# Two attention mixers of a two-layer encoder: logits, transposes and PV as separate steps, normalisation on ScalarE, alternating dilated slot pairs

## The chip, the core and the metric

The kernel runs on one core of a Trainium2 chip. The metric is the device time of one execution in microseconds. The kernel before takes 2126.91 us, the median of 3 runs (2126.51 to 2127.47).

The engines are named as in the profile: PE is TensorE (PEld its weight loads), DVE is VectorE, ACT is ScalarE, POOL is GpSimd, and SP is SyncE, whose queue issues nearly all DMAs.

## The reference

512 tokens of width 1024 go through two layers, everything in float32:

```python
for i in range(DEPTH):                                    # DEPTH = 2
    h = h + 0.5 * swiglu(rmsnorm(h, norm_ffn1[i]), ...)    # width 2816
    hn = rmsnorm(h, norm_mix[i])
    if i % 2 == 0: h = h + ab_mixer(hn, ...)               # layer 0
    else:          h = h + c_mixer(hn, ...)                # layer 1
    h = h + 0.5 * swiglu(rmsnorm(h, norm_ffn2[i]), ...)
    gate = sigmoid(rmsnorm(h, norm_ple[i]) @ w_ple_gate[i])
    h = h + gate * (p[i] @ w_ple_proj[i])
return rmsnorm(h, norm_final)
```

The mixer of layer 0 has two parts. Part A has 12 query heads on 4 key heads (64 wide), with rotary positions; a query sees the keys at a distance of at most 128, and each head has one further logit (a sink) in its softmax denominator. Part B has 4 slots, and each slot has three groups of dilated attention: distance up to 64 at stride 1, up to 256 at stride 4, and up to 1024 at stride 16. The outputs of the three groups of a slot are merged by their softmax denominators. The mixer of layer 1 is a neighbourhood attention with 16 heads: the tokens form a grid of 8 rows and 64 columns, and a query sees 8 x 16 grid cells, with a learned bias for each offset.

## The kernel before

**Layout and precision.** Activations lie with the features on the 128 partitions and the 512 tokens along the free dimension. Every float32 product of a weight matrix is made of three matmuls: operands are split into a high and a low part (`split`, lines 120 to 122: ScalarE copies the high part, VectorE or GpSimd subtracts it to get the low part), and `mm3` (lines 142 to 144) or lines 322 to 324 multiply high by high, high by low and low by high. A weight unit of 128 x 1024 is loaded on SyncE's queue and split in the same way (`unit`, lines 129 to 137).

**Buffers.** Long-lived tiles of 128 x 512 float32 come from the pool `act` with 59 buffers, short-lived ones from `tmp` with 8. PSUM has 3 banks `mm` for projections, 2 banks `sc` for scores, 2 banks `tr` for transposes and 1 bank `ob` for the PV output of a head. A tile is given out when a buffer of its pool is free, and it is free when its last reader is done.

**A head of the banded kind** (part A, and the stride-1 group of part B). The four query blocks of 128 tokens are b = 0 to 3. Block b sees the key blocks of `window(b)`, so blocks 0 and 3 have 256 keys and blocks 1 and 2 have 384. `scores` (lines 418 to 431) makes two matmuls a block and one VectorE instruction that scales, adds the mask and takes the row maximum. `a_soft` (559 to 573) then has ScalarE take the exponentials with their sums (line 568), VectorE add the sink and take the reciprocal (569, 570), and VectorE multiply every block by it (572). `windows_pv` (362 to 371) goes through the four key blocks x: it transposes the two or three logit blocks that see x (line 349, into one `tr` bank), splits the result (lines 121 and 122, ScalarE and VectorE), and makes the two PV matmuls of x (359 and 360). `half_sum` (677 to 683) adds the two halves of the output.

**The dilated part** goes by two pairs of slots. `b_steps` (575 to 675) has for a pair: `soft(0)` and `soft(1)` for its two slots (the stride-1 group as above, and the groups of stride 4 and 16 by residues, matmuls of line 598, exponentials of line 608); `merge`, which gathers the maxima and sums of both slots with 32 small copies (617 and 634), works out the merge weights and multiplies all 16 logit blocks of the pair by them on VectorE (line 638); `pv_r`, the transposes and PV of the residue groups (647 and 653); and `pv_n(0)`, `pv_n(1)`, the stride-1 group's transposes and PV.

**The neighbourhood mixer** goes by 8 head pairs: `c_soft` (785 to 812) makes scores, bias, exponentials and normalisation (VectorE, line 811); `c_pv` (814 to 836) twice transposes four blocks into one bank, splits them and makes their PV matmuls.

**The order of the work.** Each mixer writes two lists. `steps` holds the attention in order. `fill` holds the projections of queries, keys and values (and two opened parts of the output projection), which are dense TensorE work. Every entry has a weight. `weave` (lines 502 to 525) goes through the steps and puts fill entries between them: an entry comes when a step at most `lead` places further on needs it, or else when the weight of the fill done so far has fallen behind that of the steps done. The result is the program order, and program order is priority: a planner at build time goes by its own costs of the instructions, gives out buffers and lets a later instruction go ahead where an earlier one is not ready; each engine then runs its queue in the fixed order that comes out. `high_priority()` moves the instructions in it ahead. In the neighbourhood mixer `lead` is 2, in the first mixer 1. A step of a head's PV follows the logits of the next head, so that the program order is logits 0, logits 1, PV 0, logits 2, PV 1, and so on. In the first mixer the two slot pairs follow one after the other, and the last projections of the second pair stand among the PV steps of the first.

Of the kernel before, what the change touches and what calls it, by code (L numbers as in the profile page):

```python
# [15 lines left out]
P = 128  # L16
T = 512
# [19 lines left out]
class Trunk:  # L37
# [3 lines left out]
    def __init__(self, ctx, tc, io):  # L41
# [6 lines left out]
        self.ap_ = pool("act", 59)  # L48
        self.tp = pool("tmp", 8)
# [40 lines left out]
    def setup(self):  # L90
# [5 lines left out]
        self.identb = self.cp.tile([P, P], BF16, name="identb")  # L96
        nc.vector.tensor_copy(self.identb, self.ident)
# [7 lines left out]
        idle = self.cp.tile([P, T], BF16, name="idle")  # L105
# [237 lines left out]
    def transposed(self, blocks):  # L343
# [6 lines left out]
        hi, lo = self.tmp(F32R), self.tmp(F32R)  # L350
# [67 lines left out]
    def scores(self, q, k, hf, b, m):  # L418
# [6 lines left out]
        e = self.act()[:, :n]  # L425
# [5 lines left out]
        return e  # L431
# [5 lines left out]
    def ab(self, k_next):  # L437
# [94 lines left out]
    def a_steps(self, gp, t, v, m_a, sink, mix):  # L532

        heads = [(hf, j) for j in range(3) for hf in range(2)]
        es, raw = {}, {}

        def soft(hf, j):
            h = 6 * gp + 3 * hf + j
            es[hf, j] = self.a_soft(t["aq", gp, j], t["ak", gp], hf, sink[:, h:h + 1], m_a)

        def pv(hf, j):
            if hf == 0:
                raw[j] = self.act()
            g = 2 * gp + hf
            o = self.obank()
            self.windows_pv(o, es[hf, j], lambda x: v["va"][x][:, g * P:(g + 1) * P])
            self.half_sum(o, slice(hf * HD, (hf + 1) * HD), raw[j])
            if hf:
                mix[3 * gp + j] = self.split_chunk(raw[j])

        steps = []
        for i in range(len(heads) + 1):
# [509 lines left out]
```

## Time and profile before

| What | Value |
|---|---|
| Median of 3 runs | 2126.91 us |
| Profiled execution, its own time | 2126.64 us |
| Span of its instructions | 2124.8 us |
| Mean granted TensorE clock | 0.995 of full |
| First mixer, about | 380 to 660 us |
| Neighbourhood mixer, about | 1470 to 1670 us |
| DMA | 202 MB, 95 GB/s in the mean |

The profile is of one execution. A row of a group of instructions reads: line of the program, engine, operation, tiles written and read, shape, count; then busy time in us and the mean of one in ns; then the engine's idle time just before them, with what ended it. Consecutive matmuls overlap in the trace, so a mean of one matmul is longer than the distance from one to the next.

### The profile page before, as it was taken

How to read it: one execution, taken by the hardware profiler on the slowest of the kernel's cores; microseconds unless marked ns; L12 is line 12 of the kernel's file. 1: busy time of each engine (PE TensorE's matmuls, PEld its weight loads, DVE VectorE, ACT ScalarE, POOL GpSimd, SP SyncE). 2: the span in 40 equal slices, each digit the busy share in tenths (PEclk: the TensorE clock that was granted, in tenths of full speed). 3: DMA queues.
4: the chain of work that ended last, by engine and by line, in shares of the span. 5: the costliest groups of instructions: out<-in, count | busy, mean ns of one | idle time of the engine just before them, and what ended most of it. 6: DMA issues, size and time to landing. Idle time of an engine off the chain costs nothing.

```text
span 2124.8 us, 25520 instructions
## 1 busy us (share of the span) xinstructions
PE 2085.4 (98%) x9950; PEld 1734.6 (82%) x9950; DVE 1132.3 (53%) x1793; ACT 783.8 (37%) x1255; POOL 352.3 (17%) x248
## 2 busy tenths in 40 slices
PE   8999999999999999999999999999999999999998
PEld 6888888777787888888888888888888888888886
DVE  6554432699786444543354555333778744553334
ACT  4332222465544333222343233223656533232232
POOL 3111101233211111101111111013222210110111
PEclk9999999999999999999999999999999999999999
DMA  5333333221223233333333322334333223323331
GB/s 171 98 99 99 95 96 98 85 75 56 65 68 92 90 99 99 99 90 96 105 97 99 99 93 93 95 97 124 105 105 102 82 90 99 99 91 96 94 107 60
DMA packets 75385, 202.02 MB, mean 95 GB/s; under 512 B 16896, under 2 KB 24576, under 8 KB 75264
## 3 DMA queue, kind: packets, MB, share of 16 engines
q1 hardware_dynamic: 74976, 200.29, 30.8%
q8 instruction: 78, 1.28, 0.3%
q14 instruction: 43, 0.35, 0.1%
q10 hardware_dynamic: 288, 0.10, 0.0%
HBM read 191.97 MB, written 2.59 MB: 92 GB/s over the span
## 4 chain that ended last, share of the span: by engine, by line
PE 89%; DVE 5%; ACT 2%; issue 1%; POOL 1%; DMA 0%; SPq 0%; DVEq 0%; POOLq 0%; ACTq 0%
PE mm L143 15%; PE mm L144 15%; PE mm L142 15%; PE sc L142 12%; PE sc L143 12%; PE sc L144 12%; PE mm L322 1%; PE mm L323 1%; PE mm L324 1%; PE tr L349 1%; PE ob L359 1%; PE ob L360 1%; PE sc L428 1%; ACT wh L121 1%; DVE act L572 1%
## 5 line engine op out<-in xcount | busy, mean ns | idle before, releaser
L121 ACT ACTIVATE wh<-wr 128x1024 fp32r<-128x1024 f32 (+1 forms) x360 | 374.6, 1042 | 995.0 <-issue 431.1
L122 DVE TENSOR_TENSOR wl<-wr,wh 128x1024 fp32r<-128x1024 f32 (+1 forms) x343 | 510.2, 1488 | 314.1 <-ACT wh L121 313.1
L143 PE MATMUL mm<-act,wh 128*128 128x512 f32 (+1 forms) x1560 | 609.7, 391 | 3.0 <-DVE act L169 2.1
L142 PE MATMUL mm<-act,wh 128*128 128x512 f32 (+1 forms) x1560 | 609.1, 391 | 1.0 <-ACT wh L121 0.6
L144 PE MATMUL mm<-act,wl 128*128 128x512 f32 (+1 forms) x1560 | 608.3, 390 | 0.5 <-DVE wl L122 0.5
L144 PE MATMUL sc<-act,wl 128*128 128x512 f32 (+1 forms) x1138 | 442.5, 389 | 0.8 <-DVE wl L122 0.8
L142 PE MATMUL sc<-act,wh 128*128 128x512 f32 (+1 forms) x1138 | 442.9, 389 | 0.0
L143 PE MATMUL sc<-act,wh 128*128 128x512 f32 (+1 forms) x1138 | 442.5, 389 | 0.0
L143 PEld LDWEIGHTS mm<-act,wh 128*128 128x128 f32 x1560 | 293.4, 188 | 64.4 <-DVE act L169 5.3
L142 PEld LDWEIGHTS mm<-act,wh 128*128 128x128 f32 x1560 | 293.3, 188 | 60.0 <-ACT act L121 1.5
L144 PEld LDWEIGHTS mm<-act,wl 128*128 128x128 f32 x1560 | 293.2, 188 | 58.4 <-DVE wl L122 1.0
L239 POOL TENSOR_TENSOR tmp<-tmp,tmp 128x512 f32<-128x512 f32 x88 | 115.2, 1309 | 818.5 <-DVE tmp L238 783.7
L144 PEld LDWEIGHTS sc<-act,wl 128*128 128x128 f32 x1138 | 213.7, 188 | 45.1 <-DVE wl L122 1.2
L143 PEld LDWEIGHTS sc<-act,wh 128*128 128x128 f32 x1138 | 213.7, 188 | 44.1
L142 PEld LDWEIGHTS sc<-act,wh 128*128 128x128 f32 x1138 | 213.6, 188 | 43.8
L238 DVE TENSOR_TENSOR tmp<-sc,R 128x512 f32<-128x512 f32 x88 | 60.8, 691 | 276.8 <-PE sc L144 276.8
L180 POOL TENSOR_TENSOR ssq<-ssq,tmp 128x512 f32<-128x512 f32 x55 | 90.2, 1639 | 552.6 <-ACT tmp L175 525.7
L236 DVE TENSOR_TENSOR tmp<-mm,R 128x512 f32<-128x512 f32 x88 | 60.8, 691 | 130.4 <-PE mm L144 127.9
L121 ACT ACTIVATE act<-tmp 128x512 fp32r<-128x512 f32 x92 | 58.3, 634 | 117.3 <-POOL tmp L239 116.2
L322 PE MATMUL mm<-wh,act 128*128 128x256 f32 x256 | 74.4, 291 | 0.3 <-DVE act L337 0.3
L323 PE MATMUL mm<-wl,act 128*128 128x256 f32 x256 | 73.9, 289 | 0.0
L324 PE MATMUL mm<-wh,act 128*128 128x256 f32 x256 | 73.8, 288 | 0.0
(142 smaller groups left out, 1621.8 us busy)
## 6 DMA issues: line engine op xcount, KB each, us to landing
wr<-in_gu_dram SPq DMA_DIRECT2D x176, 512.0 KB, 3.5
wr<-in_dn_dram SPq DMA_DIRECT2D x64, 512.0 KB, 3.5
wr<-in_dn_dram SPq DMA_DIRECT2D x32, 384.0 KB, 3.1
wr<-in_qk_ab_dram SPq DMA_DIRECT2D x20, 512.0 KB, 3.5
wr<-in_plg_dram SPq DMA_DIRECT2D x16, 512.0 KB, 3.5
wr<-in_qk_c_dram SPq DMA_DIRECT2D x16, 512.0 KB, 3.7
act<-act SPq DMA_DIRECT2D x40, 128.0 KB, 2.2
wr<-in_v_ab_dram SPq DMA_DIRECT2D x8, 512.0 KB, 3.8
```

Source lines behind the costliest of these rows:

```text
L121: self.nc.scalar.activation(hi, src, AF.Copy)
L122: (lo_eng or self.nc.vector).tensor_tensor(lo, src, hi.bitcast(F32), op=ALU.subtract)
L142: mm(out, stat[0], mov[0], start=start, stop=False)
L143: mm(out, stat[0], mov[1], start=False, stop=False)
L144: mm(out, stat[1], mov[0], start=False, stop=stop)
L180: eng.tensor_tensor(self.acc, self.acc, sq, op=ALU.add)
L236: nc.vector.tensor_tensor(t1, pgu[0], R, op=ALU.mult)
L238: nc.vector.tensor_tensor(t2, pgu[1], R, op=ALU.mult)
L239: nc.gpsimd.tensor_tensor(t2, t1, t2, op=ALU.mult)
L322: nc.tensor.matmul(ps[b], xh, h, start=first, stop=False, skip_group_check=True)
L323: nc.tensor.matmul(ps[b], xh, l, start=False, stop=False, skip_group_check=True)
L324: nc.tensor.matmul(ps[b], xl, h, start=False, stop=last, skip_group_check=True)
```

## The change

**Normalisation.** In `a_soft` and in `merge` the multiplication of each logit block moves from VectorE (`tensor_scalar_mul`) to ScalarE (`activation` with Copy and a scale column). The neighbourhood mixer's stays on VectorE.

**Three steps.** `windows_pv` is taken apart. `windows_tr` transposes and splits key blocks in groups, block 1 alone, block 2 alone, and blocks 0 and 3 together in one bank, and puts the parts into `act` tiles; `windows_pv` is left with the eight PV matmuls. For a head of part A the program order is now: groups 1 and 2 of head n-1, logits of head n, the last group of head n-1, PV of head n-1. `c_pv` is taken apart in the same way into `c_tr` and `c_pv`, with the parts still in `tmp`.

**Dilated pairs.** The steps of the two pairs are interleaved by hand. Part A and part B now form one list (`ab_steps`), woven with `lead=2`.

**Buffers.** The four logit blocks of a banded head share three `act` tiles (`places`), the pool `act` has 58 buffers and `tmp` 10. A constant that nothing read (`identb`) is gone, and the zeros for the matmuls that warm up the clock share the space of another tile.

```diff
-        self.ap_ = pool("act", 59)
-        self.tp = pool("tmp", 8)
+        self.ap_ = pool("act", 58)
+        self.tp = pool("tmp", 10)
...
-        self.identb = self.cp.tile([P, P], BF16, name="identb")
-        nc.vector.tensor_copy(self.identb, self.ident)
...
-        idle = self.cp.tile([P, T], BF16, name="idle")
+        idle = self.small("R", [P, T], BF16, bufs=1)
...
-    def transposed(self, blocks):
+    def transposed(self, blocks, place=None):
...
-        hi, lo = self.tmp(F32R), self.tmp(F32R)
+        place = place or self.tmp
+        hi, lo = place(F32R), place(F32R)
...
-    def windows_pv(self, o, es, vcol):
-
-        for x in range(NB):
-            qb = range(*self.window(x))
+    GROUPS = ((1,), (2,), (0, 3))
+
+    def windows_tr(self, es, parts, groups):
+
+        for g in groups:
             blocks = []
-            for b in qb:
-                off = (x - self.window(b)[0]) * P
-                blocks.append(es[b][:, off:off + P])
-            hi, lo = self.transposed(blocks)
-            self.pv(o[:, qb[0] * P:(qb[-1] + 1) * P], vcol(x), (hi, lo), x == 0, x == NB - 1)
+            for x in g:
+                for b in range(*self.window(x)):
+                    off = (x - self.window(b)[0]) * P
+                    blocks.append(es[b][:, off:off + P])
+            hi, lo = self.transposed(blocks, self.act)
+            at = 0
+            for x in g:
+                n = P * len(range(*self.window(x)))
+                parts[x] = (hi[:, at:at + n], lo[:, at:at + n])
+                at += n
+
+    def windows_pv(self, o, parts, vcol):
+
+        xs = [x for g in self.GROUPS for x in g]
+        for x in xs:
+            lo, hi = self.window(x)
+            self.pv(o[:, lo * P:hi * P], vcol(x), parts[x], x == xs[0], x == xs[-1])
...
+    def places(self):
+
+        a, b, c = self.act(), self.act(), self.act()
+        return [c[:, 0:2 * P], a[:, 0:3 * P], b[:, 0:3 * P], c[:, 2 * P:]]
...
-        steps = (self.a_steps(0, t, v, m_a, sink, mix) + self.a_steps(1, t, v, m_a, sink, mix)
-                 + self.b_steps(0, t, v, m_b0, m_br, mix) + self.b_steps(1, t, v, m_b0, m_br, mix))
...
-        self.weave(steps, fill, after={("o", 0): 26})
+        steps, begin = self.ab_steps(t, v, (m_a, m_b0, m_br), sink, mix)
+        self.weave(steps, fill, lead=2, after={("o", 0): begin})
...
+        two, last = self.GROUPS[:2], self.GROUPS[2:]
...
+        for i, k in enumerate(heads):
+            prev = heads[i - 1] if i else None
             if i:
-                steps.append((["va"], 1, lambda h=heads[i - 1]: pv(*h)))
-        return steps
+                steps.append(([], .3, lambda k=prev: tr(k, two)))
+            steps.append(([("ak", k[0]), ("aq", k[0], k[2])], 1, lambda k=k: soft(k)))
+            if i:
+                steps.append(([], .2, lambda k=prev: tr(k, last)))
+                steps.append((["va"], 1, lambda k=prev: pv(k)))
+        k = heads[-1]
+        b0, b1 = b
+        steps += [([], .3, lambda: tr(k, two)), b0["soft", 0], ([], .2, lambda: tr(k, last)), (["va"], 1, lambda: pv(k)),
+                  b0["soft", 1], b0["merge"], b1["soft", 0], b0["r"], b0["tr", 0], b1["soft", 1]]
+        begin = len(steps)
+        steps += [b0["pv", 0], b1["merge"], b0["tr", 1], b0["pv", 1], b1["r"], b1["tr", 0], b1["pv", 0],
+                  b1["tr", 1], b1["pv", 1]]
+        return steps, begin
...
-            nc.vector.tensor_scalar_mul(es[b], es[b], rd[:, b:b + 1])
+            nc.scalar.activation(es[b], es[b], AF.Copy, scale=rd[:, b:b + 1])
...
-                        nc.vector.tensor_scalar_mul(e, e, ww)
+                        nc.scalar.activation(e, e, AF.Copy, scale=ww)
...
+        def tr_n(hf):
+            self.windows_tr(c["e0", hf], c.setdefault(("parts", hf), {}), self.GROUPS[:2])
...
-        return [(qk, 1.5, lambda: soft(0)), (qk, 1.5, lambda: soft(1)), ([], 2, merge),
-                ([("vr", sp)], .7, pv_r), (["vb"], 1.2, lambda: pv_n(0)), ([], 1.2, lambda: pv_n(1))]
+        steps = {"merge": ([], .5, merge), "r": ([("vr", sp)], 1, pv_r)}
+        for hf in range(2):
+            steps["soft", hf] = (qk, 1.5, lambda hf=hf: soft(hf))
+            steps["tr", hf] = ([], .3, lambda hf=hf: tr_n(hf))
+            steps["pv", hf] = (["vb"], 1, lambda hf=hf: pv_n(hf))
+        return steps
...
+                    steps.insert(-1, ([], .3, lambda k=(m, hm): tr.__setitem__(k, self.c_tr(es[k]))))
                     steps.append(([("v", m // 2)], 1, lambda m=m, hm=hm: pv(m, hm)))
...
+    def c_tr(self, es):
+        key = lambda b, i: es[b][:, i * P:(i + 1) * P]
+        parts = []
+        for g in (1, 3):
+            last = (key(g, 1), key((g + 1) % NB, 0)) if g == 1 else (key(0, 0), key(3, 1))
+            parts.append(self.transposed([key(g - 1, 1), key(g, 0), *last]))
+        return parts
```

By the rule of `weave`, the program order of the dilated part is now: logits of pair 0's first slot, the values of pair 0's residues, the last of part A's PV, six projections of pair 1 in a row, logits of pair 0's second slot, `merge` 0, logits of pair 1's first slot, `pv_r` 0, transposes, logits of pair 1's second slot, PV, `merge` 1, and the rest of pair 0 and pair 1. Before it was: pair 0 complete, with pair 1's projections between its steps from `merge` on, then pair 1 complete.

More of the change, by code (lines that the diff above doesn't have):

```diff
@@ L416, in rope, with scores @@
         return o
-    def scores(self, q, k, hf, b, m):
+    def places(self):
+        a, b, c = self.act(), self.act(), self.act()
+        return [c[:, 0:2 * P], a[:, 0:3 * P], b[:, 0:3 * P], c[:, 2 * P:]]
+    def scores(self, q, k, hf, b, m, e):
         nc = self.nc
@@ L530, in split_chunk, with ab_steps, soft, tr @@
         return hi, lo
[L532 to L537, printed above, removed]
-            h = 6 * gp + 3 * hf + j
-            es[hf, j] = self.a_soft(t["aq", gp, j], t["ak", gp], hf, sink[:, h:h + 1], m_a)
-        def pv(hf, j):
+    def ab_steps(self, t, v, masks, sink, mix):
+        m_a, m_b0, m_br = masks
+        heads = [(gp, hf, j) for gp in range(2) for j in range(3) for hf in range(2)]
+        es, parts, raw = {}, {}, {}
+        def soft(k):
+            gp, hf, j = k
+            h = 6 * gp + 3 * hf + j
+            es[k] = self.a_soft(t["aq", gp, j], t["ak", gp], hf, sink[:, h:h + 1], m_a)
+        def tr(k, groups):
+            self.windows_tr(es[k], parts.setdefault(k, {}), groups)
+        def pv(k):
+            gp, hf, j = k
@@ L542, in pv @@
             if hf == 0:
-                raw[j] = self.act()
+                raw[gp, j] = self.act()
             g = 2 * gp + hf
             o = self.obank()
-            self.windows_pv(o, es[hf, j], lambda x: v["va"][x][:, g * P:(g + 1) * P])
-            self.half_sum(o, slice(hf * HD, (hf + 1) * HD), raw[j])
+            self.windows_pv(o, parts[k], lambda x: v["va"][x][:, g * P:(g + 1) * P])
+            self.half_sum(o, slice(hf * HD, (hf + 1) * HD), raw[gp, j])
             if hf:
-                mix[3 * gp + j] = self.split_chunk(raw[j])
+                mix[3 * gp + j] = self.split_chunk(raw[gp, j])
@@ L551, in a_steps @@
+        two, last = self.GROUPS[:2], self.GROUPS[2:]
         steps = []
-        for i in range(len(heads) + 1):
-            if i < len(heads):
-                steps.append(([("ak", gp), ("aq", gp, heads[i][1])], 1, lambda h=heads[i]: soft(*h)))
+        b = [self.b_steps(sp, t, v, m_b0, m_br, mix) for sp in range(2)]
+        for i, k in enumerate(heads):
+            prev = heads[i - 1] if i else None
             if i:
-                steps.append((["va"], 1, lambda h=heads[i - 1]: pv(*h)))
@@ L562, in a_soft @@
         mx, neg, den, snk, rd = (st[:, i, :] for i in range(5))
-        es = [self.scores(q, k, hf, b, (m_a, mx[:, b:b + 1])) for b in range(NB)]
+        es = self.places()
+        for b in range(NB):
+            self.scores(q, k, hf, b, (m_a, mx[:, b:b + 1]), es[b])
         nc.vector.tensor_scalar(neg, mx, s, -1.0, op0=ALU.max, op1=ALU.mult)
@@ L588, in soft @@
             ng = self.small("ng_b", [P, 2, 4])
-            e0 = [self.scores(t["bq", sp, 0], t["bk", sp, 0], hf, b, (m_b0, st[:, 0, 0, b:b + 1])) for b in range(NB)]
+            e0 = self.places()
+            for b in range(NB):
+                self.scores(t["bq", sp, 0], t["bk", sp, 0], hf, b, (m_b0, st[:, 0, 0, b:b + 1]), e0[b])
             rows = slice(hf * HD, (hf + 1) * HD)
@@ L662, in pv_n @@
             rows = slice(hf * HD, (hf + 1) * HD)
+            self.windows_tr(c["e0", hf], c["parts", hf], self.GROUPS[2:])
             o = self.obank()
-            self.windows_pv(o, c["e0", hf], lambda x: v["vb"][x][:, s * P:(s + 1) * P])
+            self.windows_pv(o, c["parts", hf], lambda x: v["vb"][x][:, s * P:(s + 1) * P])
             x0 = self.tmp()
@@ L769, in c @@
                     steps.append(([], 0, lambda hf=hf: parts(range(1, 3) if hf else range(1))))
-        steps += [([], 0, lambda: parts([KC - 2])), ([], 1, lambda: pv(KC - 1, 1))]
+        steps += [([], 0, lambda: parts([KC - 2])),
+                  ([], .3, lambda: tr.__setitem__((KC - 1, 1), self.c_tr(es[KC - 1, 1]))),
+                  ([], 1, lambda: pv(KC - 1, 1))]
         fill += [(("o", m), PART, lambda m=m: self.out_part(io["o_c"], m, mix, range(KC - 2))) for m in range(OPEN)]
@@ L812, in c_soft, with c_pv @@
         return es
-    def c_pv(self, hd, hf, es, vs, raw):
+    def c_tr(self, es):
[5 more added lines that the diff above has]
+        return parts
+    def c_pv(self, hd, hf, parts, vs, raw):
         nc = self.nc
@@ L817, in c_pv @@
         o = self.obank()
-        key = lambda b, i: es[b][:, i * P:(i + 1) * P]
-        for g in (1, 3):
-            last = (key(g, 1), key((g + 1) % NB, 0)) if g == 1 else (key(0, 0), key(3, 1))
-            pt = self.transposed([key(g - 1, 1), key(g, 0), *last])
+        for g, pt in zip((1, 3), parts):
             for i in range(2):
```

5 lines of the change are left out of this document (2 added, 3 removed).

## The prediction

> **What bounds the kernel now.** I read the page first, then the stretches, the clock, the waits of TensorE, and last the groups of instructions inside the first mixer.
>
> ```profile
> span 2124.8 us, 25520 instructions
> PE 2085.4 (98%) x9950; PEld 1734.6 (82%) x9950; DVE 1132.3 (53%) x1793; ACT 783.8 (37%) x1255; POOL 352.3 (17%) x248
> ```
>
> TensorE is busy for 98% of the span, so a change that leaves the matmuls as they are can win back only idle or slow-clocked TensorE time. The table by stretches (columns: stretch, length, then busy time and count for PE, PEld, DVE, ACT, POOL; clock; DMA share; GB/s) says where that is.
>
> ```profile
> 380.00:660.00 280.00, 261.18 (x1510) 219.23 (x1511) 224.14 (x590) 144.82 (x346) 72.59 (x51) 0.98 0.20 61
> 690.00:1470.00 780.00, 779.91 (x3459) 645.30 (x3459) 353.11 (x366) 242.66 (x300) 100.99 (x75) 1.00 0.32 98
> 1470.00:1670.00 200.00, 195.27 (x1205) 171.24 (x1204) 147.48 (x425) 119.59 (x261) 49.19 (x30) 1.00 0.33 94
> ...
> 394.80:398.20 3.40, 2.93 (x11) 2.93 (x12) 2.28 (x7) 0.06 (x1) 0.00 (x0) 0.50 0.03 11
> 548.40:555.20 6.80, 6.24 (x25) 5.70 (x25) 3.71 (x15) 6.05 (x21) 0.00 (x0) 0.50 0.00 0
> 568.90:572.30 3.40, 2.94 (x8) 2.46 (x9) 3.37 (x8) 0.00 (x0) 1.89 (x3) 0.50 0.15 48
> ...
> 562.00:568.90 6.90, 4.74 (x21) 3.57 (x20) 6.01 (x39) 4.36 (x12) 0.00 (x0) 1.00 0.40 118
> ```
>
> The feed-forward stretch (690 to 1470) has nothing to give. The first mixer (A heads and dilated slots, 380 to 660) idles 280.0 - 261.2 = 18.8 us and holds three stretches at half clock, 13.6 us together; the neighbourhood mixer (1470 to 1670) idles 4.7 us. In the first mixer VectorE is busy 224 of 280 us and ScalarE only 145. The waits of TensorE (who waited for whom: us in all, times, longest), first mixer, then the second:
>
> ```profile
> PE tr L349 <- DVE act L572: 5.1, 6, 1.6
> PE tr L647 <- DVE act L638: 4.3, 2, 2.6
> PE ob L360 <- DVE tmp L122: 2.8, 3, 1.6
> PE sc L428 <- DVE act L270: 2.5, 1, 2.5
> PE tr L206 <- POOL rcol L190: 1.4, 1, 1.4
> ...
> PE ob L359 <- ACT tmp L121: 2.1, 7, 0.4
> PE ob L360 <- DVE tmp L122: 1.7, 3, 0.6
> ```
>
> The first two rows are transposes that wait for VectorE to normalise a head's logits; the third, and both of the second mixer, are PV matmuls that wait for the split of transposed blocks. L428 and L206 belong to the mixer's start, which the change leaves alone.
>
> **The normalisation goes to ScalarE.** Rows by form, in the first mixer and (the two of 128x512) the second:
>
> ```profile
> L572 DVE TENSOR_SCALAR act<-act,st_a 128x256 f32<-128x256 f32 x24 | 16.5, 687 | 0.2
> L572 DVE TENSOR_SCALAR act<-act,st_a 128x384 f32<-128x384 f32 x24 | 9.4, 418 | 0.0
> L638 DVE TENSOR_SCALAR act<-act,w_b 128x256 f32<-128x256 f32 x24 | 8.2, 387 | 0.1
> L638 DVE TENSOR_SCALAR act<-act,w_b 128x384 f32<-128x384 f32 x8 | 3.6, 453 | 0.0
> ...
> L568 ACT ACTIVATE act<-act,st_a 128x256 f32<-128x256 f32 x24 | 12.0, 500 | 6.9 <-DVE st_a L564 6.9
> L568 ACT ACTIVATE act<-act,st_a 128x384 f32<-128x384 f32 x24 | 14.5, 603 | 0.0
> ...
> L122 DVE TENSOR_TENSOR tmp<-tr,tmp 128x384 fp32r<-128x384 f32 x32 | 17.4, 551 | 6.4 <-ACT tmp L121 6.4
> L122 DVE TENSOR_TENSOR tmp<-tr,tmp 128x256 fp32r<-128x256 f32 x32 | 13.5, 421 | 9.4 <-ACT tmp L121 9.0
> L121 ACT ACTIVATE tmp<-tr 128x384 fp32r<-128x384 f32 x32 | 15.4, 486 | 14.5 <-PE tr L349 14.3
> L121 ACT ACTIVATE tmp<-tr 128x256 fp32r<-128x256 f32 x32 | 12.2, 382 | 18.6 <-PE tr L349 18.2
> ...
> L121 ACT ACTIVATE tmp<-tr 128x512 fp32r<-128x512 f32 x32 | 18.2, 597 | 3.5 <-PE tr L349 3.2
> L122 DVE TENSOR_TENSOR tmp<-tr,tmp 128x512 fp32r<-128x512 f32 x32 | 20.9, 681 | 1.1 <-ACT tmp L121 1.1
> ```
>
> VectorE loses 16.5 + 9.4 + 8.2 + 3.6 = 37.7 us. No row shows a Copy with a scale column on such a tile; the nearest is the exponential of the same tiles, 0.500 and 0.603 us, which I take for the 48 blocks of 128x256 and 32 of 128x384: 24.0 + 19.3 = 43.3 us more for ScalarE. Three transposed groups a head (384, 384, 512 columns) replace four (256, 384, 384, 256), in 16 heads: the ScalarE halves go from 16 x 1.736 = 27.8 to 16 x 1.569 = 25.1 us, the VectorE halves from 31.1 to 28.5. VectorE ends near 224.1 - 37.7 - 2.6 = 184 us and ScalarE near 144.8 + 43.3 - 2.7 = 185 us, both well under TensorE's 261. Cover therefore exists on average; what counts is order.
>
> VectorE's mean for the narrow block, 687 ns, is over that for the wide one. The timeline at one long wait shows why:
>
> ```profile
> 516.73 2.37 POOL L122 TENSOR_TENSOR wl<-wr,wh 128x1024 fp32r<-128x1024 f32 x1 [3.48 <-ACT wh L121]
> ...
> 517.16 3.01 DVE L572 TENSOR_SCALAR act<-act,st_a 128x256 f32<-128x256 f32 x4
> ...
> 519.40 0.68 PE L349 MATMUL tr<-ident,act 128*128 128x128 f32 x4 [1.32 <-DVE act L572]
> ```
>
> Four normalisations took 3.01 us while GpSimd split a weight, and the transposes stood 1.32 us. [...]
>
> The new wait: the Copy waits on ScalarE for VectorE's reciprocal or merge weights. Behind it in ScalarE's queue stand the splits of other heads' transposes and of weight units, for which TensorE waits. I charge 0.60 - 0.45 = 0.15 us (wide copy against VectorE's wide form in L638) at each of the 6 + 2 places where TensorE waited for a normalisation: 1.2 us. Bounds: 0, and all 9.4 us of those waits kept.
>
> **Three steps a head.** Between a head's transposes and its PV now stand the next head's eight score matmuls and a second transposed group, so the split has run when PV comes: the waits of 2.8 us, and 2.1 + 1.7 = 3.8 us in the second mixer, go; bounds none and all. No matmul is added. The second mixer holds four tmp buffers from the transposes to PV; two more are there, so I cost it at nothing, and a held buffer would show as a wait of the transposes, up to the 3.8 again.
>
> **Dilated pairs alternate.** The merge of pair 0 now has the scores of pair 1, and the other way round, beside it. The 4.3 us before L647 go, and with them the idle stretch of 562 to 568.9 (6.90 - 4.74 = 2.2 us), after which the clock was halved for 3.4 us; that is 1.7 us more. The other late stretch, 548.4 to 555.2, follows the scores of pair 0 and I leave it: bounds 0 and 3.4 us.
>
> Six projections of pair 1 now come in one run before the last scores of pair 0: 6 x 24 matmuls at 780 / 3459 = 0.2255 us are 32.5 us of TensorE work that once stood among pair 0's steps. Their six weight loads on SyncE's queue come at the feed-forward's pace (98 GB/s there), the copies of the stacked keys in that queue wait for ScalarE as before, and GpSimd gets the same rotations; I cost the move past these queues at nothing; were loads late, a wait for the weight split would show.
>
> **Buffers.** Counting act tiles along the program order, before needs at most 56 of 59. After needs 64 of 58 when the residue values of pair 0 are built, 63 at pair 0's second scores and 62 at pair 1's: six parts a head outlive the transposes and both pairs are open. So work must be held back there until a tile is free. No row shows such a wait; the nearest is the longest wait of TensorE here, 2.6 us. I charge two, 5.2 us; bounds 0, and the rival below.
>
> **Start.** One cast (L97) goes.
>
> ```profile
> 5.97 0.23 DVE L97 CAST identb<-ident 128x128 bf16<-128x128 f32 x1 [4.70 <-DMA ident<-in_ident_dram]
> ...
> 6.85 1.23 DVE L122 TENSOR_TENSOR wl<-wr,wh 128x1024 fp32r<-128x1024 f32 x1
> ...
> 5.76 1.06 ACT L121 ACTIVATE wh<-wr 128x1024 fp32r<-128x1024 f32 x1
> ```
>
> The weight's low half starts at 6.85, right when its high half ends (6.82), so the cast costs nothing; without that cover it is 0.23 us.
>
> **The sum.** Gone: 5.1 + 4.3 + 2.8 + 3.8 + 1.7 = 17.7 us. Back: 1.2 + 5.2 = 6.4. Net -11.3. The profiled execution took 2126.64 us (span 2124.8 and 1.8 around it), so 2115.3; the median, 2126.91, is 0.3 above it: 2116 us.
>
> **Rivals.**
>
> *More comes free.* All idle time of both mixers but the 2.5 + 1.4 at the start goes, 18.8 + 4.7 - 3.9 = 19.6 us, and both late half-clock stretches, (6.8 + 3.4) / 2 = 5.1: -24.7, 2102 us. For it: three loaded engines all stay under 190 of 261 us. Against: the buffer count.
>
> *The waits change their name.* The order that runs is the planner's, and transposes already ran among other heads' matmuls; TensorE then waits for the Copy on ScalarE as it did for VectorE, in the first mixer nothing is won, and half of the 3.8 in the second: 2125 us. For it: ScalarE's queue is in order and gets 43 us more.
>
> *Slower: tiles run out in the dilated part.* The projections of pair 1 take the last act tiles, pair 0's second scores wait for one, and neither the merge nor the fill can go on. Uncovered then is a chain worked out from these rows:
>
> ```profile
> L608 ACT ACTIVATE act<-act,ng_b 128x256 f32<-128x256 f32 x24 | 11.9, 504 | 4.9 <-DVE ng_b L605 4.9
> L608 ACT ACTIVATE act<-act,ng_b 128x384 f32<-128x384 f32 x8 | 4.8, 605 | 0.0
> L608 ACT ACTIVATION_READ_ACCUMULATOR act<-act,ng_b 128x1 f32 x32 | 6.2, 194 | 0.0
> ...
> L617 DVE COPY s_b<-st_b 32x4 f32<-32x4 f32 x32 | 7.0, 220 | 3.6 <-ACT act L608 3.2
> L634 DVE COPY w_b<-w_b 32x2 f32<-32x2 f32 x32 | 5.1, 160 | 0.5
> ```
>
> a quarter of the exponentials, 22.9 / 4 = 5.7, half of the small copies, 6.1, and one Copy, 0.5: 12.3 us, for both pairs 24.6, and 1.7 us of half clock after each. With -17.7 + 1.2 that is +11.5: 2138 us. It turns the result from the point where TensorE's waits in the dilated part pass 16.5 us.
>
> **How the numbers follow.** Chances: the forecast 0.49 (its own range 2109 to 2122), more 0.17, renamed 0.20, slower 0.14. A measurement of this kernel can tell about 0.2%, 4.3 us. Faster by over that: 0.47 + 0.17 + 0.04 = 0.68 (forecast, more, renamed); within: 0.02 + 0.15 + 0.01 = 0.18; slower: 0.01 + 0.13 = 0.14 (renamed and slower; within: forecast, renamed, slower). The range, 2102 to 2130, cuts off about 0.13 of slower cases above and 0.06 below.
>
> **What would show it.** Right: no TensorE wait for a normalisation over about 1 us in all; VectorE near 184 and ScalarE near 185 us in the first mixer; no half clock after pair 0's merge; less than 1 us of PV waits in the second mixer. Wrong: waits of scores or projections for a tile that PV or transposes free, or of TensorE for ScalarE's Copy, over 6 us together; or new half-clock stretches behind 580 us.

## The result, and the profile after

The changed kernel takes 2138.36 us (median of 4 runs, 2136.76 to 2139.46), the kernel before, beside it, 2127.11 us: a ratio of 1.0053, 95% interval 1.0035 to 1.007. It is slower by some 11 us, where the forecast was 11 us faster. The page of the changed kernel:

```profile
span 2135.0 us, 25498 instructions
PE 2088.5 (98%) x9950; PEld 1736.6 (81%) x9950; DVE 1102.6 (52%) x1696; ACT 816.0 (38%) x1319; POOL 349.7 (16%) x248
```

VectorE lost 30 us of work, ScalarE took 32, TensorE is busy for the same 98%, and the span is 10.2 us longer. Where, the table by stretches says (stretch, length, busy time and count for PE, PEld, DVE, ACT, POOL; clock; DMA share; GB/s). First the kernel before, then the changed one:

```profile
380.00:540.00 160.00, 148.03 (x841) 124.98 (x842) 136.94 (x337) 89.88 (x214) 53.64 (x38) 0.99 0.21 62
540.00:580.00 40.00, 36.11 (x222) 30.65 (x220) 28.55 (x104) 20.22 (x54) 8.71 (x6) 0.87 0.15 47
580.00:640.00 60.00, 57.46 (x343) 48.62 (x339) 47.34 (x132) 25.49 (x60) 10.24 (x8) 1.00 0.24 79
640.00:680.00 40.00, 39.59 (x202) 31.54 (x199) 27.84 (x34) 21.03 (x34) 8.36 (x5) 1.00 0.31 92
```

```profile
380.00:540.00 160.00, 149.92 (x845) 125.24 (x845) 109.92 (x265) 105.11 (x235) 52.93 (x38) 0.99 0.22 65
540.00:580.00 40.00, 39.06 (x211) 33.13 (x211) 26.44 (x54) 23.33 (x53) 14.47 (x10) 1.00 0.22 73
580.00:640.00 60.00, 53.71 (x345) 45.58 (x345) 41.55 (x158) 33.94 (x92) 3.88 (x3) 1.00 0.19 60
640.00:680.00 40.00, 30.66 (x154) 23.33 (x153) 21.44 (x25) 21.94 (x40) 5.51 (x3) 0.87 0.09 22
```

The heads (to 540) win 1.9 us of busy time. From 540 to 580 the changed kernel is ahead too: 39.06 us busy against 36.11, at full clock where the kernel before had 0.87. All of it and more is lost behind 580: 57.46 - 53.71 = 3.7 us, and 39.59 - 30.66 = 8.9 us in the last 40 us of the dilated part, where now the clock is 0.87. The waits of TensorE from 380 to 690 us (us, times, longest), after:

```profile
PE mm L140 <- ACT act L119: 5.4, 2, 3.3
PE tr L347 <- DVE act L120: 2.6, 4, 1.2
...
PE tr L347 <- ACT act L607: 0.8, 3, 0.5
```

The wait of the transposes for a normalisation is down from 5.1 to 0.8 us (L572 is now L607), and the 4.3 us behind the merge are not in the whole list. In their place TensorE stands at the output projection (L140), waiting for a split of ScalarE. The timeline of TensorE at the last PV of the dilated part shows it; before and after:

```profile
652.35 0.39 PE L360 MATMUL ob<-tmp,act 128*128 128x256 f32 x1
...
656.08 0.73 PE L142 MATMUL mm<-act,wh 128*128 128x512 f32 x2 [0.38 <-ACT act L121]
```

```profile
662.80 0.41 PE L359 MATMUL ob<-act,act 128*128 128x256 f32 x1
666.54 1.16 PE L140 MATMUL mm<-act,wh 128*128 128x512 f32 x2 [3.32 <-ACT act L119]
```

The chain behind that PV (its halves added, gathered, split) takes 3.7 us in both. Before, matmuls of the output projection that needed only finished chunks ran beside it and left 0.38 us bare; after, TensorE ran none there, and 3.32 us were bare. The same from another side: the first and last start of the dilated residue scores, and of the value projections, which are the other cover of this part (before, then after):

```profile
L598 PE MATMUL sc<-act,act x64: 272/272/373, 545.6 to 624.1; 64*128 64x128 f32 x64
L324 PE MATMUL mm<-wh,act x128: 277/283/415, 388.1 to 627.3; 128*128 128x256 f32 x128
```

```profile
L635 PE MATMUL sc<-act,act x64: 272/272/373, 554.1 to 626.0; 64*128 64x128 f32 x64
L322 PE MATMUL mm<-wh,act x128: 278/283/415, 388.0 to 609.9; 128*128 128x256 f32 x128
```

Before, values were still projected at 627 us, 25 us ahead of the last PV; after, the last was at 610, 53 us ahead of it. The last residue scores come only 1.9 us later than before, the last PV 10.4 us later: from the one to the other it takes 36.8 us instead of 28.3.

Of the signs that the prediction named, VectorE is busy for 185.6 us from 380 to 660 (near 184 was forecast) and ScalarE for 174.0 (near 185). A Copy with a scale column took 0.500 us on 128x256 and 0.602 on 128x384, as assumed; the longest of the heads' 48 took 0.610 us, where VectorE's longest at L572 had taken 2.480 before. The sign of being wrong that came true is the half clock behind 580 us; the last section shows it.

In the second mixer the waits of PV are gone but for 0.2 us, and the scores wait instead (from 1470 to 1700 us, after):

```profile
PE sc L848 <- ACT tmp L119: 2.6, 2, 1.3
PE sc L848 <- DMA act<-act: 1.3, 1, 1.3
```

That is 3.9 us, where PV had waited 3.8.

### The profile page after: what moved, and what is told of

It reads as the page before. It is cut to its first block, busy times and chain, and to the rows that moved or that the text cites. A ratio compares the mean times of both kernels' runs of the same rounds, so it can differ in the third digit from the quotient of the medians.

```text
span 2135.0 us, 25498 instructions
## 1 busy us (share of the span) xinstructions
PE 2088.5 (98%) x9950; PEld 1736.6 (81%) x9950; DVE 1102.6 (52%) x1696; ACT 816.0 (38%) x1319; POOL 349.7 (16%) x248
## 4 chain that ended last, share of the span: by engine, by line
PE 89%; DVE 4%; ACT 3%; issue 1%; POOL 1%; DMA 0%; SPq 0%; DVEq 0%; ACTq 0%; POOLq 0%
PE mm L140 15%; PE mm L142 15%; PE mm L141 15%; PE sc L140 12%; PE sc L142 12%; PE sc L141 12%; PE tr L347 1%; PE mm L322 1%; PE mm L321 1%; PE mm L320 1%; PE sc L848 1%; PE ob L358 1%; PE ob L359 1%; PE sc L444 1%; ACT act L675 0%
## 5 line engine op out<-in xcount | busy, mean ns | idle before, releaser
L140 PE MATMUL mm<-act,wh 128*128 128x512 f32 (+1 forms) x1560 | 609.9, 391 | 9.2 <-ACT act L119 5.6
L140 PE MATMUL sc<-act,wh 128*128 128x512 f32 (+1 forms) x1138 | 443.6, 390 | 0.1
L140 PEld LDWEIGHTS mm<-act,wh 128*128 128x128 f32 x1560 | 293.7, 188 | 70.4 <-ACT act L119 7.0
L140 PEld LDWEIGHTS sc<-act,wh 128*128 128x128 f32 x1138 | 214.0, 188 | 44.4 <-PE sc L635 0.2
```

The source lines that it names most:

```text
L140: mm(out, stat[0], mov[0], start=start, stop=False)
```

## The experiments

In the diffs "-" is the line of the kernel that the text names and "+" the experiment's. Times are medians; each ratio is to the kernel before, run beside the experiment on the same chip (2125.8 to 2126.6 us). The change was measured on another occasion, beside 2127.1 us, so a difference between an experiment and the change can be off by some 1.3 us, and a smaller one tells nothing.

**The parts one by one.** First the order of the pairs: the changed kernel with pair 0 complete ahead of pair 1.

```diff
-                  b0["soft", 1], b0["merge"], b1["soft", 0], b0["r"], b0["tr", 0], b1["soft", 1]]
+                  b0["soft", 1], b0["merge"], b0["r"], b0["tr", 0], b0["pv", 0], b0["tr", 1], b0["pv", 1]]
...
-        steps += [b0["pv", 0], b1["merge"], b0["tr", 1], b0["pv", 1], b1["r"], b1["tr", 0], b1["pv", 0],
+        steps += [b1["soft", 0], b1["soft", 1], b1["merge"], b1["r"], b1["tr", 0], b1["pv", 0],
```

> The changed kernel, with the two dilated pairs one after the other again (pair 1's scores come after pair 0's last PV; three steps, ScalarE normalisation and buffers as changed). Bare tail: in the changed kernel both pairs' last chains stand behind the last projection, and TensorE loses some 12 us more than before between 630 and 680 us; with the pairs in sequence pair 1's projections lie beside pair 0's merge again, so the time falls by 9 to 13 us, to 2125 to 2129. Late splits on ScalarE: the 16 copies of each merge are still there, the time falls by 4 us at most, to 2134 to 2138. Tile shortage: the need along the program order falls to about 60 of 58, and the time falls by some 5 us.

Measured 2138.81 us, ratio 1.0065 (1.005 to 1.008). Undoing the alternation gives nothing back. It is not the order of the kernel before, though: with `lead=2` the weave puts the last value projection ahead of pair 1's second softmax, where `lead=1` had it behind. In this trace the last value matmul starts at 626.4 us and the last residue scores at 634.8, so nothing of the projections is left behind them.

The changed kernel with the merge's multiplications on VectorE again:

```diff
-                        nc.scalar.activation(e, e, AF.Copy, scale=ww)
+                        nc.vector.tensor_scalar_mul(e, e, ww)
```

> The changed kernel, with the 32 blocks of the two merges multiplied on VectorE again. Late splits on ScalarE: the 2 us wait of the output projection for the split that stands behind seven merge copies goes, and a half-clock stretch of 1.7 us with it, perhaps the same at the other merge: 4 to 8 us less, 2130 to 2134. Bare tail: the chain only changes its engine, within 2 us of the changed kernel, 2136 to 2140.

Measured 2129.18 us, ratio 1.0017 (1.0008 to 1.0027): 9.2 us less than the change, most of its loss. ScalarE's timeline at the second merge of the changed kernel shows what stands behind it:

```profile
642.53 3.12 ACT L675 ACTIVATE act<-act,w_b 128x256 f32<-128x256 f32 x7
645.55 0.61 ACT L119 ACTIVATE act<-act 128x512 fp32r<-128x512 f32 x1
646.19 1.08 ACT L686 ACTIVATE tmp<-tr 128x512 f32<-128x512 f32 x2
```

The split at 645.55, for which TensorE stood 2.05 us, and the evacuations of the transposes (L686) are queued behind seven copies.

The changed kernel with the heads' normalisation on VectorE again, as the line before, at L607:

> The changed kernel, with the 48 blocks of the banded heads normalised on VectorE again. If the ScalarE normalisation is worth the 5.1 us that the transposes waited for it before, the time rises by 3 to 5 us, to 2141 to 2143. If the three steps alone hide that wait, or if ScalarE's waits took its place, it stays within 2 us, 2136 to 2140.

Measured 2142.71 us, ratio 1.0088 (1.0071 to 1.0105): 4.3 us slower than the change. TensorE's first row of waits is then

```profile
PE tr L347 <- DVE act L607: 9.5, 10, 1.7
```

so ScalarE is the better place for this multiplication in the new order. By the time of the whole kernel, ScalarE is worth 4.3 us for the heads by this run, and VectorE 9.2 us for the merge by the one ahead of it.

The kernel before with the three steps of the second mixer, the changed pools and the start without the cast, alone:

```diff
-        self.ap_ = pool("act", 59)
-        self.tp = pool("tmp", 8)
+        self.ap_ = pool("act", 58)
+        self.tp = pool("tmp", 10)
...
+                    steps.insert(-1, ([], .3, lambda k=(m, hm): tr.__setitem__(k, self.c_tr(es[k]))))
                     steps.append(([("v", m // 2)], 1, lambda m=m, hm=hm: pv(m, hm)))
```

> The kernel before, with only the neighbourhood mixer in three steps, and the changed buffers (58 act, 10 tmp). The prediction's 3.8 us there: 2123 to 2124. From the two traces the mixer as a whole wins only about 0.5 us, so 2126 to 2127.5 if the trace is right, the rest going to waits of scores.

Measured 2125.92 us, ratio 0.9999 (0.999 to 1.0009): nothing. TensorE's two rows of waits at the scores come back here, with 2.6 and 1.2 us.

The kernel before with one multiplication on ScalarE: the merge's (L638), the heads' (L572), and both.

```diff
-            nc.vector.tensor_scalar_mul(es[b], es[b], rd[:, b:b + 1])
+            nc.scalar.activation(es[b], es[b], AF.Copy, scale=rd[:, b:b + 1])
```

> The kernel before with one edit alone: the 32 blocks of the merges are multiplied on ScalarE. On VectorE the 16 blocks of a merge take 4.6 us while ScalarE evicts the first transposes beside them; on ScalarE they take 7.1 us and the evictions stand behind them in the same queue, some 4 us more on the chain of each merge. Late splits on ScalarE: 4 to 9 us more, 2130 to 2135. If it needs the new order to hurt: 2125 to 2128.

> The kernel before with one line changed: the normalisation of the heads (L572) goes from VectorE to ScalarE; order, pools and the merge stay. Theory A, the normalisation is a gain of its own, worth what it is worth in the changed kernel (2142.7 - 2138.4 = 4.3 us): near 2122 us, and the 5.1 us of transposes behind L572 shrink to under 2 us. Theory B, in the old order, where the transposes stand right behind the scores, the wait only changes its name: 2126 us, within 2 us of before, and TensorE waits some 5 us for ScalarE at L572.

> The kernel before with both normalisations (L572, L638) on ScalarE; order and pools stay. Theory A: the gain of the heads (4 us) and that of the merge multiplies in the old order (2124.9 against 2126, so 1 us) add up: near 2121 us, which would be faster than both kernels. Theory B, ScalarE gets late when it has all 43 us more: 2126 to 2130 us, and waits of TensorE for ScalarE over 8 us in the first mixer.

Measured: merge 2124.87 us, ratio 0.9996 (0.9986 to 1.0006); heads 2125.93 us, 1.0 (0.999 to 1.001); both 2124.59 us, 0.9993 (0.9984 to 1.0002). So the move to ScalarE by itself costs nothing and gains nothing that can be told. With the heads' multiplication moved, in the old order, the waits of TensorE (in a profile of 2128.22 us, the slowest of its ten runs) are

```profile
PE sc L428 <- DVE act L270: 3.9, 2, 2.6
PE sc L428 <- DVE st_a L429: 2.5, 2, 2.1
...
PE tr L349 <- ACT act L572: 0.7, 1, 0.7
```

where the kernel before had 5.1 us at L349 and 2.5 at L428 behind L270: the wait went from the transposes to the scores, which wait for VectorE (L270, L429) and not for the Copy.

The changed kernel with the steps of a head put together again, and with two more act tiles:

```diff
+            steps.append(([("ak", k[0]), ("aq", k[0], k[2])], 1, lambda k=k: soft(k)))
             if i:
                 steps.append(([], .3, lambda k=prev: tr(k, two)))
-            steps.append(([("ak", k[0]), ("aq", k[0], k[2])], 1, lambda k=k: soft(k)))
-            if i:
...
-        self.ap_ = pool("act", 58)
-        self.tp = pool("tmp", 10)
+        self.ap_ = pool("act", 60)
+        self.tp = pool("tmp", 8)
```

> The changed kernel with the three steps of a head put together again in the first mixer: both transposes and the PV of a head stand behind the next head's scores, as in the kernel before; the rest (both normalisations on ScalarE, alternation, lead of two) stays. Theory A, the splitting into three steps gave nothing in the first mixer: 2138 us, within 3 us of after. Theory B, splitting hides the waits for the splits as the prediction had it (2.8 us): 2141 us. Theory C, splitting takes other heads' scores out of reach of the order and is itself a part of the loss: 2134 us or less.

> The changed kernel with 60 act tiles and 8 tmp tiles in place of 58 and 10. Theory A, the prediction's rival in which act tiles run out in the dilated part: two more tiles take a part of its price back, 2130 to 2135 us, and the half clock behind 640 us goes or moves. Theory B, act tiles hold nothing back: 2138 us, within 2 us of after (in the second mixer two tmp tiles fewer may cost up to 2 us).

Measured 2137.19 us, ratio 1.0055 (1.004 to 1.007), and 2137.94 us, ratio 1.0057 (1.0042 to 1.0072). Neither gives the time back. By the prediction's count six tiles were missing, so two more don't rule out tiles by themselves; runs further down do more.

**Lead one**, instead of two, in the changed kernel; with the merge on VectorE besides; and with both and the pairs in sequence:

```diff
-        self.weave(steps, fill, lead=2, after={("o", 0): begin})
+        self.weave(steps, fill, lead=1, after={("o", 0): begin})
```

> The changed kernel with the first mixer woven with lead 1 instead of 2. Cover spent early: with lead 2 the last values (96 matmuls, some 11 us of TensorE) and pair 1's projections stand one step earlier in the program order than with lead 1, ahead of pair 0's second scores and of its merge; with lead 1 the last scores run sooner and more dense work is left for the tail: 3 to 6 us less, 2132 to 2135. If the lead does not matter: 2137 to 2139.

> The changed kernel (pairs alternate), the merges multiplied on VectorE and lead 1. If the merge copies (9.6 us) and the lead add up: 2123 to 2126. If the lead does nothing: 2128 to 2130.

> Pairs in sequence, the merges multiplied on VectorE and lead 1: what is left of the change is three steps, ScalarE normalisation of the banded heads, buffers. If the whole loss came from the merge copies and from cover spent early by lead 2, the tail is as in the kernel before and the head part is 2 to 4 us better: 2121 to 2124. If the three steps cost in the dilated part themselves: 2127 to 2131.

Measured 2132.73 us, ratio 1.0034 (1.0021 to 1.0047); 2130.61 us, 1.0023 (1.0014 to 1.0033); 2128.91 us, 1.0013 (1.0004 to 1.0023). How early the projections are forced matters (5.6 us), and the merge's engine costs 2.1 us here where it cost 9.2 with a lead of two. In the last two runs, which differ by the order of the pairs alone, alternation is the slower by 1.7 us: the transposes of the residue groups wait 10.7 us for the merge with it (L684 behind L675) and 5.6 us without. No part undone brought all of the time back, and the merge's engine, which brought back the most, costs nothing in the old order. So the next suspect was what they share: the list of projections, paced along new steps.

**The cover moved.** The changed kernel with the values vb held back until the first dilated softmax, step 46, has been issued:

```diff
-        self.weave(steps, fill, lead=2, after={("o", 0): begin})
+        self.weave(steps, fill, lead=2, after={("o", 0): begin, "vb": 47})
```

> The changed kernel with the values vb held back until the first dilated softmax has been issued, where the kernel before has them. The first residue scores came at 545.6 us before and at 554.1 after. Theory 'late start', the later start of the dilated part sets the later end: the start comes back by some 8 us and the time falls to about 2130 us. Theory 'what stands ahead of the last scores', the end is set by the last dilated scores of pair 1 and by what TensorE has left behind them: these do not move, so 2138 us within 2 us, with the first residue scores near 546 us all the same.

Measured 2146.07 us, ratio 1.0097 (1.008 to 1.0114): 7.7 us slower than the change, which neither theory had. The residue scores start at 552.7 us instead of 554.1, so the dilated part hardly began earlier, and this run does not test the theory of the late start. Its stretches:

```profile
380.00:540.00 160.00, 149.72 (x845) 124.74 (x844) 109.61 (x263) 104.90 (x234) 52.82 (x38) 0.99 0.22 67
540.00:580.00 40.00, 34.12 (x181) 28.39 (x179) 18.71 (x49) 20.67 (x50) 10.42 (x9) 0.91 0.17 51
580.00:640.00 60.00, 55.72 (x344) 47.90 (x343) 42.73 (x132) 30.75 (x76) 7.02 (x5) 0.97 0.22 68
640.00:680.00 40.00, 30.81 (x161) 22.83 (x160) 21.05 (x55) 24.19 (x54) 0.00 (x0) 0.87 0.04 14
```

TensorE, without vb beside the last heads, falls from 39.06 to 34.12 us busy between 540 and 580, and the end stays as bare as it was.

The kernel before with one move in its list, pair 1's residue values ahead of pair 1's projections:

```diff
         fill = (a0[:2] + proj_v("va", 0) + a0[2:] + a1 + proj_b(0) + proj_v("vb", 1) + proj_v(("vr", 0), 2)
-                + proj_b(1) + proj_v(("vr", 1), 3))
+                + proj_v(("vr", 1), 3) + proj_b(1))
```

> The kernel before with one move in its list of projections: the residue values of pair 1 come ahead of pair 1's six projections, so that 12 us more of TensorE work (an estimate from mean durations of matmuls) stand ahead of the last dilated scores and no value projection behind them. Nothing else of the change is in it. Theory 'what stands ahead of the last scores': the end of the dilated part moves back as in the changed kernel, 2132 to 2138 us. Theory 'the order of projections doesn't matter while TensorE is busy 98%': 2126 us within 2 us.

Measured 2137.15 us, ratio 1.0053 (1.0038 to 1.0068): the loss of the change, in a kernel that has nothing of the change. Its stretches, and its residue scores and value projections:

```profile
380.00:540.00 160.00, 148.05 (x840) 124.84 (x839) 136.77 (x337) 89.79 (x214) 53.62 (x38) 0.99 0.21 63
540.00:580.00 40.00, 35.58 (x276) 32.64 (x275) 27.13 (x104) 20.93 (x57) 3.69 (x2) 0.96 0.21 66
580.00:640.00 60.00, 59.21 (x293) 48.77 (x292) 41.32 (x97) 23.39 (x55) 14.58 (x11) 1.00 0.25 75
640.00:680.00 40.00, 30.71 (x155) 22.93 (x154) 27.85 (x61) 16.36 (x29) 6.00 (x3) 0.87 0.08 27
```

```profile
L598 PE MATMUL sc<-act,act x64: 272/272/374, 545.8 to 633.9; 64*128 64x128 f32 x64
L324 PE MATMUL mm<-wh,act x128: 274/283/415, 387.9 to 581.8; 128*128 128x256 f32 x128
```

The last 40 us are those of the changed kernel, 30.71 against 30.66 us busy, 0.87 and 0.87 of the clock. The residue scores start where they did before (545.6 us), so the loss needs no late start. It comes about in another way than in the changed kernel: here the last scores are 9.8 us later than before and the last PV follows them after 26.5 us; there the scores were 1.9 us later and the way to the last PV was 8.5 us longer. What the two have in common is that no projection is left beside the last merge and PV steps.

The other way round: the changed kernel with the value projections behind pair 1's dilated softmaxes; for this, pair 1's projections move ahead and its second softmax comes before pair 0's residue PV. Then the same with the merge on VectorE.

```diff
-        fill = (a0[:2] + proj_v("va", 0) + a0[2:] + a1 + proj_b(0) + proj_v("vb", 1) + proj_v(("vr", 0), 2)
-                + proj_b(1) + proj_v(("vr", 1), 3))
+        fill = (a0[:2] + proj_v("va", 0) + a0[2:] + a1 + proj_b(0) + proj_b(1) + proj_v("vb", 1)
+                + proj_v(("vr", 0), 2) + proj_v(("vr", 1), 3))
...
-        self.weave(steps, fill, lead=2, after={("o", 0): begin})
+        self.weave(steps, fill, lead=2, after={("o", 0): begin, "vb": 53})
...
-                  b0["soft", 1], b0["merge"], b1["soft", 0], b0["r"], b0["tr", 0], b1["soft", 1]]
+                  b0["soft", 1], b0["merge"], b1["soft", 0], b1["soft", 1], b0["r"], b0["tr", 0]]
```

> The changed kernel with pair 1's six projections ahead of the values vb and vr0, both of pair 1's dilated softmaxes ahead of pair 0's residue PV, and the values held back until these softmaxes are issued; both normalisations stay on ScalarE, lead two, alternation. Some 27 us less of TensorE work stand ahead of the last scores in program order. Theory 'what stands ahead of the last scores': the merges and the PV steps have three value projections as cover, the last dilated PV comes about 10 us earlier than 662.8, and the time falls to about 2128 us. Theory 'ScalarE's queue', the sixteen copies of a merge on ScalarE cost by themselves: 2135 to 2139 us.

> As the kernel with the values last, and the multiplications of the merge on VectorE. Theory 'what stands ahead of the last scores': 2129 - 9 = 2120 us or somewhat above, faster than both kernels. Theory 'ScalarE's queue' explains the 9 us of the merge alone and the order nothing: 2129 us.

Measured 2128.71 us, ratio 1.0017 (1.0008 to 1.0027), and with VectorE 2132.72 us, 1.0031 (1.002 to 1.0043). The first came out as expected, 9.7 us under the change, with ScalarE's merge in place. The second was to be 9 us lower still and is 4.0 us higher: that part of the theory fell. The stretches of the first, then of the second:

```profile
380.00:540.00 160.00, 150.51 (x779) 120.99 (x779) 110.75 (x268) 103.65 (x232) 56.70 (x43) 0.99 0.22 68
540.00:580.00 40.00, 35.78 (x214) 31.33 (x213) 28.04 (x62) 20.04 (x48) 12.88 (x8) 0.96 0.16 53
580.00:640.00 60.00, 55.07 (x395) 50.36 (x393) 36.27 (x148) 44.19 (x115) 1.29 (x1) 0.94 0.16 52
640.00:680.00 40.00, 39.14 (x208) 31.23 (x208) 27.82 (x32) 20.46 (x33) 8.35 (x5) 1.00 0.32 104
```

```profile
380.00:540.00 160.00, 150.59 (x766) 122.11 (x767) 109.22 (x262) 101.29 (x227) 54.89 (x41) 0.97 0.22 66
540.00:580.00 40.00, 35.71 (x205) 30.49 (x204) 28.15 (x62) 19.98 (x43) 14.54 (x9) 0.96 0.18 56
580.00:640.00 60.00, 53.39 (x391) 47.79 (x391) 45.70 (x184) 32.23 (x91) 1.42 (x2) 0.97 0.18 58
640.00:680.00 40.00, 39.22 (x215) 31.16 (x214) 25.68 (x31) 20.01 (x33) 6.97 (x4) 1.00 0.27 85
```

The end is covered again, 39.14 us at full clock; what is bare now is the stretch of the softmaxes. The second differs from the first among the heads, ahead of both merges: 0.97 of the clock for 0.99, which is 3.2 us. From 540 to 680, where the merges are, idle time and the clock's loss (as in the table below) add up to 15.2 us in the first and 15.1 in the second. So these profiles show no price of the merge's engine in this order.

In two more kernels a part of the values is put into the stretch of the softmaxes: with a lead of one and no hold (vb and vr0 between pair 1's two softmaxes), and, with lead two, vb behind pair 0's softmaxes and vr0 behind pair 1's (the diff is of this one, against the kernel with the values last):

```diff
-        self.weave(steps, fill, lead=2, after={("o", 0): begin, "vb": 53})
+        self.weave(steps, fill, lead=2, after={("o", 0): begin, "vb": 50, ("vr", 0): 53})
```

> As the kernel with the values last (2128.7 us, both normalisations on ScalarE), without the hold and with a lead of one: the values vb and vr0 come between the two dilated softmaxes of pair 1, vr1 later. In the values-last kernel the end is covered, and the idle TensorE has moved to the dilated softmaxes, 560 to 600 us. Theory 'cover has to be spread over the whole dilated part': with vb and vr0 in that place 2122 to 2127 us. Theory 'a fixed loss of the new order': 2129 us within 2 us.

> As the kernel with the values last, but of the three value projections one (vb) comes behind pair 0's softmaxes, and two (vr0, vr1) are held behind pair 1's. Theory 'cover has to be spread over the whole dilated part': idle time between 560 and 600 us falls, no half clock behind 640 us, 2120 to 2126 us. Theory 'a fixed loss of the new order': 2129 us within 2 us.

Measured 2127.37 us, ratio 1.0006 (0.9997 to 1.0015), a little over what was expected, and 2124.29 us, ratio 0.999 (0.9981 to 1.0), 14 us under the change. The second is the fastest kernel with the new order, level with the old order with both multiplications on ScalarE (2124.59). Its stretch from 580 on has full clock and 1.7 us less idle time than with the values last, and the end stays covered (39.19 us busy from 640 to 680, at full clock):

```profile
580.00:640.00 60.00, 56.75 (x432) 51.78 (x430) 38.04 (x151) 45.87 (x119) 1.30 (x1) 1.00 0.20 62
```

For the changed kernel and the two that lose as it does, TensorE's idle time and its clock account for most of the difference in span. Idle is 300 less the busy sum; the clock's loss is (1 - clock) times the length, summed; both are set against the kernel before (18.8 us idle, 6.8 us by the clock).

| kernel | idle more | clock more | sum | span more |
| --- | --- | --- | --- | --- |
| changed | 7.8 | 0.0 | 7.8 | 10.2 |
| before, vr1 first | 7.6 | 1.6 | 9.2 | 10.3 |
| changed, vb held | 10.8 | 5.4 | 16.2 | 19.4 |

The clock is given to 0.01, which makes 1.5 us either way; the remainder lies outside these stretches or in that rounding.

## Why the prediction was wrong

**The step that failed** is "six projections of pair 1 in one run", costed at nothing. I looked at their weight loads and queues, which are not what counts; the prediction had said itself that what counts is order. By the weave's rule, projections are placed by due time and by the share of the steps' weight that has passed, and the new steps, weights and lead put vb ahead of pair 0's first softmax, and vr0 and all six projections of pair 1 ahead of its second. What then remains beside the merges, the transposes and the PV steps of both pairs is one value projection and the opened output chunks. TensorE idles and drops its clock there: between 640 and 680 it is idle 8.9 us more than before, and the clock of 0.87 costs another 5.2 us, while the stretches to 580 give a part back; the span grows by 10.2 us. Two runs show it from both sides: the old kernel with one value projection moved ahead loses 11.0 us, and the changed one with the values moved behind the softmaxes (and pair 1's steps with them) wins 9.7.

In the changed kernel the missing cover does not make the loss alone. With the merge on VectorE the projections stand as early, and 3.4 us are lost. On ScalarE the copies lengthen the chain behind the last scores (36.8 us to the last PV, 32.3 with the merge on VectorE). That is free where projections run beside it (in the old order, and with the values last), and dear where none is left.

**"Gone: 4.3 + 1.7", the merges covered by alternation:** wrong. The waits at L647 did go in the changed kernel, but in the two runs that differ by alternation alone it is 1.7 us the slower, with the longer wait behind the merge (10.7 against 5.6 us); pair 1's scores are a small cover beside what the projections had been.

**"Gone: 5.1", the heads' normalisation:** the wait fell to 0.8 us, and VectorE's busy time in the heads (to 540) from 136.94 to 109.92, yet the heads won 1.9 us. In the old order the rival "the waits change their name" had the outcome, though not the engine: the scores waited instead, for VectorE and not for the Copy, and the time stood still. In the new order ScalarE is worth 4.3 us.

**"Gone: 2.8" and "3.8", three steps a head:** wrong by their whole size. Undone in the first mixer, the time falls by 1.2 us, which is within the uncertainty; alone in the second they change nothing (2125.92 against 2125.81 us), since the scores wait there 3.9 us where PV had waited 3.8.

**"Back: 1.2", the hand-over to ScalarE:** near for the heads (0.8 us, in three waits where six were reckoned). For the merge I had left out the price of ScalarE's order in a stretch without cover: 9.2 us as the change stands, 2.1 with a lead of one. Where projections are left beside the merges no price shows: with the values last, the kernel with the merge on ScalarE is the faster by 4.0 us, a difference that lies ahead of the merges, and in the old order there is nothing between them.

**"Back: 5.2", waits for act tiles, and the slower rival:** the rival named the place (the dilated part), the sign and almost the time (2138), and by its cause it is not borne out, so the agreement of its number is luck. No run shows the 5.2 us. Two tiles more gave 0.4 us; the values-last kernel, with the same 58 tiles and pair 1's projections earlier still, is 9.7 us faster; and the old kernel with its 59 tiles shows the same loss. That some tile was waited for somewhere is not excluded.

**Open:** why, in the values-last order, the kernel with the merge on VectorE runs at a lower clock among the heads, ahead of the merges. How much of the changed kernel's loss comes from the early projections, how much from vb and vr0, and how much from ScalarE's copies, no run took apart.

## What to carry over

When TensorE is nearly full (98% here), matmuls that need not wait for the chain are the cover for every chain of small steps, and there is only so much of them: a change of step order, weights or lead spends that cover, so list for each serial stretch which independent matmuls will still be left when it comes, above all for the last. A wait that is removed counts as won only once the next row of the waits has been looked for, and it is worth trying a one-line move of cover before a restructuring. Work that moves to another engine's queue has no fixed price: the same thirty-two copies cost 9.2 us in a bare stretch and nothing that could be told under cover.

## What the chip showed beside

The clock halved here also after stretches in which TensorE was far from idle. In the changed kernel the three stretches at half clock behind 640 us, then the 3.4 us ahead of each, are:

```profile
646.10:649.50 3.40, 3.29 (x19) 2.46 (x19) 0.69 (x1) 1.15 (x3) 0.00 (x0) 0.51 0.00 0
659.80:663.20 3.40, 3.25 (x11) 2.44 (x11) 1.02 (x2) 0.60 (x1) 0.00 (x0) 0.50 0.00 0
666.60:670.00 3.40, 3.40 (x8) 2.72 (x9) 1.17 (x2) 0.98 (x2) 0.00 (x0) 0.50 0.00 0
```

```profile
642.70:646.10 3.40, 1.47 (x8) 0.78 (x6) 1.74 (x2) 3.40 (x8) 0.00 (x0) 1.00 0.00 0
656.40:659.80 3.40, 1.55 (x10) 0.89 (x9) 2.44 (x4) 1.47 (x3) 0.00 (x0) 1.00 0.02 5
663.20:666.60 3.40, 0.08 (x2) 0.07 (x1) 1.93 (x3) 1.22 (x2) 0.00 (x0) 1.00 0.00 0
```

TensorE was busy for 1.47, 1.55 and 0.08 of 3.4 us, and the next 3.4 us ran at half clock, 1.7 us lost each. In the kernel before, the half clock from 548.4 to 555.2 follows a stretch that is busier still:

```profile
545.00:548.40 3.40, 2.70 (x20) 2.15 (x18) 2.38 (x13) 0.00 (x0) 0.69 (x1) 1.00 0.00 0
```

So half clock followed stretches of 3.4 us that were busy for 2, 43, 46 and 79%, while 633.7 to 637.1 us of the kernel before, busy for 1.76 us (52%), had full clock behind it: the share of busy time alone does not tell when it comes. The wait of 2.05 us at 646 us and the 1.7 us lost to the half clock right behind it come to 3.75 us, nearly twice the wait.
